# RG-LRU gates in rows of their own, the attention's mixed rows in its idle buffers, the residual rows loaded one projection sooner

## The chip, the cores and the metric

The kernel runs on one core of a Trainium2 chip. The metric is the time of one execution on the device, in microseconds (us). The core's engines each run their own queue of instructions in order and meet through semaphores: PE (TensorE, the matmuls), DVE (VectorE), ACT (ScalarE), POOL (GpSimd) and SP (SyncE, which here issues nearly all DMAs).

## The reference

One inference step of a small decoder trunk: 2 layers, model width 1024, one prompt of 1024 tokens and 8 sample tokens that go on from caches. Each layer is one input projection, three mixers side by side, one output projection and a layer norm. In short:

```python
proj = x @ w_in                               # q, k, v, gates, lru, ssd inputs
q, k, v, g_att, x_lru, g_lru, z_ssd, xbc, dt = split(proj)
br_a = sliding_window_attention(q, k, v, sinks) * silu(g_att)     # 512 wide
xl   = causal_conv(x_lru)
r, ig = sigmoid(xl @ w_a + b_a), sigmoid(xl @ w_x + b_x)          # 8 blocks of 96
log_a = -8 * softplus(-lam) * r
h    = scan(exp(log_a), sqrt(1 - exp(2 * log_a)) * ig * xl)       # RG-LRU
br_b = h * silu(g_lru)                                            # 768 wide
y    = ssd_scan(silu(causal_conv(xbc)), softplus(dt + bias)) + d * x_ssd
br_c = rms_norm(y * silu(z_ssd))                                  # 768 wide
x    = layer_norm(alpha * x + concat(br_a, br_b, br_c) @ w_out)
```

## The kernel before

All activations stand transposed: channels on the 128 partitions, tokens along the row. The work goes in four steps, layer 0 and 1 by two halves of the prompt: half 0 has 512 tokens, half 1 has 512 and the 8 samples (520, computed as two chunks of 260). Float32 products are made of three matmuls with split operands (`mac3`, L301 to L303: high by high, high by low, low by high). A weight block comes in by `W8`: a load (L250), a split on ACT (L226 in half 0, L253 in half 1) and a low part on POOL (L227), or, in half 1, a load of the low part kept from half 0 (L252).

A step projects, block by block of 128 channels (`project`): k and v, dt, then four times q, the attention gate and two SSD blocks, then eight SSD blocks, then the RG-LRU blocks as XL 0 to 2, GL 0 to 2, XL 3 to 5, GL 3 to 5 (`lru_project`; GL is the gate path, whose tanh is L345 and product L346 in `gate_silu`). Attention, SSD and RG-LRU themselves run as streams of small pieces between the projections (`spawn`, `pump`). Their results, the mixed rows, go to DRAM (`mixd`, four groups of 512 channels). `out_proj` reads them group by group in the order attention (0), SSD (3), RG-LRU (1), the rest (2): `load_mix` loads four rows of a group and splits each into a high part (L233, ACT) and a low part (L234, DVE). For each group PE makes eight out tiles, and DVE adds each to the residual rows r (L1024).

The tiles in question: a u tile is 4 rows of 520 floats on each partition (`u_tile`, pool of NU = 10), used for x, for conv results (xc, xb, zc), for gates, for mixed rows, for r and for the norm. Tiles "qa" (4 of them) hold the split queries, "sp" (4) scores and transposed probabilities; both lie idle when the attention of a step has ended. In half 1, `ssd_stream` also takes the 8 samples through the SSD one by one (`sample`): B and C of two samples come broadcast as "bb" (L685), the state as h0 (L687, 2 buffers), ACT scales (L689), POOL updates the state (L690, L691), DVE reduces it (L694). `finish` (L595, L597) makes an SSD block's gated result, `squares` (L608 on ACT, L609 on DVE) its sum of squares for the norm, which ends with a ones matmul (L731). The gate matmuls of the RG-LRU are L455, its scan L471, and its gated result L483.

The order of each engine's instructions is fixed when the kernel is built, by the scheduler of the tile framework, from the order of the code, the sizes of the pools and its own estimates of time; a tile of a pool can be written only when the last reader of the slot's former tile is done. On SP all loads and stores stand in one such order.

Of the kernel before, what the change touches and what calls it, by code (L numbers as in the profile page):

```python
# [12 lines left out]
F32R = mybir.dt.float32r  # L13
AF = mybir.ActivationFunctionType
# [3 lines left out]
P = 128  # L18
# [3 lines left out]
NS = 8  # L22
# [12 lines left out]
NH = 5  # L35
NS2 = 4
NE = 5
NU = 10
NQ = 2
ND = 4  # L40
NA = 3
# [9 lines left out]
def tile_trunk(ctx, tc, outs, x_t, cache_k, cache_v, st_lru_conv, st_ssd_conv, st_ssd_h, w_in, w_dt, w_out,  # L51
# [23 lines left out]
    def u_tile(dt=F32):  # L75
        return up.tile([P, 4, WMAX], dt, tag="u", name="u")
# [4 lines left out]
    def wtile(shape, tag, bufs=1, dt=F32):  # L81
        return wk.tile(shape, dt, tag=tag, name=tag, bufs=bufs)
# [259 lines left out]
    def gate_silu(ps, W, out):  # L342

        th = wtile([P, WMAX], "ev", NE)
        S.activation(sv(th[:, :W], W), pv(ps, W), AF.Tanh, scale=0.5)  # L345
        V.scalar_tensor_tensor(sv(out, W), sv(th[:, :W], W), 1.0, pv(ps, W), op0=ALU.add, op1=ALU.mult)  # L346
# [60 lines left out]

    def lru_project(st, l, half, x, j, what):  # L410

        W = HALF + NS * half
        if what == 0:
            xc = st["xc", j] = u_tile()
        else:
            gt = st["gt", j] = u_tile()
        for i in range(3):
            t = 3 * j + i
            if what == 0:
                ps = project(l, x, W, B_XL + t)  # L420
                conv(ps, half, W, lru_p[:, t, :], l * LS + 32, past_l[:, l, t, :], halo_l[:, t, :], xc[:, i, :W],
                     last_l[:, :, t])
                dma(xc[32 * i:32 * i + 32, 3, :W], xc[96:P, i, :W])
                if half and t == 5:
                    spawn("tail", rows_out(last_l.rearrange("p c t -> p (c t)"), 66, (
                        (0, 18, p_lru_conv[l, 0].rearrange("c (t p) -> (c t) p", p=P)),
                        (18, 66, s_lru_conv[l, :, 2, :].rearrange("b (t p) -> b t p", p=P)))), 2)
            else:
                ps = project(l, x, W, B_GL + t)
                gate_silu(ps, W, gt[:, i, :W])  # L430
            st["lru", j, what, i] = True

    def lru_stream(st, l, half, mixrows):
# [3 lines left out]
        for j in range(2):  # L437
# [5 lines left out]
            for i in range(3):  # L443
                while ("lru", j, 1, i) not in st:
                    yield 1
                t = 3 * j + i
                gate = st["gt", j][:, i, :W]
                r, ig = wtile([P, WMAX], "hb", NH), wtile([P, WMAX], "hb", NH)
                for gi, dst in ((0, r), (1, ig)):
                    for cs in chunks(W):  # L450
# [134 lines left out]
    def ssd_stream(st, l, half, mixrows):  # L585
# [81 lines left out]
        def sample(g):  # L667
# [12 lines left out]
            ysum = wtile([P, 3, NS], "ysum")  # L680
            heads = slice(6 * g, 6 * g + 6)
            for b in range(NS):
                if b % 2 == 0:
                    bb = wtile([P, 2, 2, P], "bb", 2)
                    dma(bb, bview(bcd, b * 2 * P, [[0, P], [1, 4 * P]]))  # L685
                h0, u = wtile([P, 3, P], "h0", 2), wtile([P, 3, P], "sd", ND)
                dma(h0, st_ssd_h[l, b, heads].rearrange("(t e) p n -> (e p) t n", e=2))  # L687
                for t in range(3):
                    S.activation(u[:, t, :], bb[:, b % 2, 0, :], AF.Copy, scale=dcols[:, 0, t, b:b + 1])  # L689
                G.tensor_tensor(h0, h0, dcols[:, 1, :, b:b + 1].to_broadcast([P, 3, P]), ALU.mult)  # L690
                G.tensor_tensor(h0, h0, u, ALU.add)  # L691
                dma(s_ssd_h[l, b, heads].rearrange("(t e) p n -> (e p) t n", e=2), h0)
                for t in range(3):
                    V.tensor_tensor_reduce(u[:, t, :], bb[:, b % 2, 1, :], h0[:, t, :], 1.0, 0.0,  # L694
                                           op0=ALU.mult, op1=ALU.add, accum_out=ysum[:, t, b:b + 1])
                yield 1
            finish(g, cs, NS, ysum)
# [113 lines left out]
    def attention_q(st, l, half, x, g):  # L811
        W = HALF + NS * half
        ps = project(l, x, W, B_Q + g)
        qa = st["qg", g] = [wtile([P, HALF], "qa", 2 * NQ, F32R) for _ in range(2)]

        def queries(q):

# [154 lines left out]


    def load_mix(half, mixd, g):
        W = HALF + NS * half
        mh, ml = u_tile(F32R), u_tile(F32R)
        for k in range(4):
            load_split(mh[:, k, :W], ml[:, k, :W], mixd[g][k * P:(k + 1) * P, :W])
        return mh, ml

    GROUPS = ((0, ("att",)), (3, ("ssd", "ssd_sub")), (1, ("lru",)), (2, ()))

    def out_proj(l, half, mixd, load_next, first):
        W = HALF + NS * half
        n = W // 2
        r = [u_tile() for _ in range(2)]
        for i in range(2):
            dma(r[i][:, :, :W], xd[l, half][512 * i:512 * i + 512, :W].rearrange("(k p) w -> p k w", p=P))
        cur = first
        for gi, (g, _) in enumerate(GROUPS):  # L990
            if gi == 1 and half == 0:
# [15 lines left out]
            for part in ((slice(HALF // 2, W), slice(0, HALF // 2)) if split_c else (None,)):  # L1007
                for op in range(4):
                    w = weights((l, g, op))
                    for oo in range(2):  # L1010
# [6 lines left out]
                            products = [pc(ps, W, c) for c in range(len(chunks(W)))]  # L1017
                        for out, cs in products:
                            for k in range(4):
                                mac3(out, w.part(k, slice(oo * P, oo * P + P)), mh[:, k, cs], ml[:, k, cs],  # L1020
                                     k == 0, k == 3)
                        ro, po = r[o // 4][:, o % 4, :W], pv(ps, W)
                        ro, po = (ro[:, part], products[0][0]) if part else (sv(ro, W), po)
# [89 lines left out]
    def step(l, half, x, load_next):  # L1113
# [24 lines left out]
        spawn("lru", lru_stream(st, l, half, mixrows))  # L1138
        if start:
            dma(ln_p, ln_cols)  # L1140
        for j in range(2):
            lru_project(st, l, half, x, j, 0)
            if j:
                drain("att")
                first = load_mix(half, mixd, 0)
            lru_project(st, l, half, x, j, 1)
        return out_proj(l, half, mixd, load_next, first)

    steps = [(l, half) for l in range(LAYERS) for half in range(2)]
    for l, half in steps:  # L1150
# [137 lines left out]
```

## Time and profile before

| | |
|---|---|
| time, median of 3 runs | 1694.64 us (1694.28 to 1696.47) |
| the profiled execution's own time | 1691.48 us |
| its span in the trace | 1689.7 us |
| PE busy | 1580.7 us (94%) |
| DVE, ACT, POOL busy | 63%, 57%, 34% of the span |
| mean bandwidth of the DMA queues | 200 GB/s |

The profiled execution is one run; a duration of the trace belongs to it and not to the median. The busy shares are means over four steps: what an engine is worth at one place is read from the waits there. PE's clock is granted at full or at half speed; the windows show it as a share of full speed.

### The profile page before, as it was taken

How to read it: one execution, taken by the hardware profiler on the slowest of the kernel's cores; microseconds unless marked ns; L12 is line 12 of the kernel's file. 1: busy time of each engine (PE TensorE's matmuls, PEld its weight loads, DVE VectorE, ACT ScalarE, POOL GpSimd, SP SyncE). 2: the span in 40 equal slices, each digit the busy share in tenths (PEclk: the TensorE clock that was granted, in tenths of full speed). 3: DMA queues.
4: the chain of work that ended last, by engine and by line, in shares of the span. 5: the costliest groups of instructions: out<-in, count | busy, mean ns of one | idle time of the engine just before them, and what ended most of it. 6: DMA issues, size and time to landing. Idle time of an engine off the chain costs nothing.

```text
span 1689.7 us, 30520 instructions
## 1 busy us (share of the span) xinstructions
PE 1580.7 (94%) x10696; PEld 1344.8 (80%) x10696; DVE 1071.8 (63%) x2118; ACT 964.2 (57%) x2066; POOL 578.5 (34%) x642
## 2 busy tenths in 40 slices
PE   8899998999989989989998999988999998989896
PEld 6677776688889888779976777656889997978896
DVE  5656667855944756774487565679436558577724
ACT  5655566733555746783256555667346656477724
POOL 4543665342010344300144436654412105352000
PEclk9999999999999999999999999999999999999999
DMA  8655554976564766687646555559866456565966
GB/s 274 192 169 162 152 173 156 316 244 200 146 190 150 216 188 200 194 291 251 198 129 194 163 162 152 153 183 306 251 213 197 157 175 199 179 209 183 310 200 207
DMA packets 210657, 337.40 MB, mean 200 GB/s; under 512 B 24116, under 2 KB 64000, under 8 KB 210456
## 3 DMA queue, kind: packets, MB, share of 16 engines
q1 hardware_dynamic: 208200, 331.27, 62.0%
q10 hardware_dynamic: 2304, 4.20, 0.7%
q8 instruction: 84, 1.38, 0.3%
q14 instruction: 69, 0.57, 0.1%
HBM read 242.76 MB, written 92.05 MB: 198 GB/s over the span
## 4 chain that ended last, share of the span: by engine, by line
PE 58%; DVE 15%; DMA 12%; ACT 7%; issue 4%; SPq 2%; POOL 2%; DVEq 0%; ACTq 0%; POOLq 0%
PE ip L301 16%; PE ip L303 16%; PE ip L302 16%; PE mm L879 2%; DMA wraw<-in_w_in_dram 2%; DMA wl<-low 2%; DVE u L360 2%; PE mm L655 1%; PE mm L850 1%; DMA acr<-acsd 1%; PE mm L868 1%; PE mm L455 1%; DVE hb L471 1%; DMA out_dram<-h 1%; DMA bb<-bcd 1%
## 5 line engine op out<-in xcount | busy, mean ns | idle before, releaser
L301 PE MATMUL ip<-u,wh 128*128 128x260 f32 (+3 forms) x2592 | 857.8, 331 | 53.4 <-DVE u L346 18.7
L303 PE MATMUL ip<-u,wl 128*128 128x260 f32 (+3 forms) x2592 | 844.1, 326 | 7.3 <-DMA wl<-low 7.1
L302 PE MATMUL ip<-u,wh 128*128 128x260 f32 (+3 forms) x2592 | 842.2, 325 | 0.0
L301 PEld LDWEIGHTS ip<-u,wh 128*128 128x128 f32 x2592 | 497.6, 192 | 114.8 <-DVE u L346 22.8
L303 PEld LDWEIGHTS ip<-u,wl 128*128 128x128 f32 x2592 | 496.3, 192 | 54.8 <-DMA wl<-low 9.4
L302 PEld LDWEIGHTS ip<-u,wh 128*128 128x128 f32 x2592 | 497.4, 192 | 38.4 <-issue 2.7
L227 POOL TENSOR_TENSOR wl<-wraw,wh 128x512 fp32r<-128x512 f32 x216 | 310.2, 1439 | 330.2 <-ACT wh L226 263.8
L253 ACT ACTIVATE wh<-wraw 128x512 fp32r<-128x512 f32 x224 | 138.1, 625 | 175.2 <-PE ip L302 138.7
L226 ACT ACTIVATE wh<-wraw 128x512 fp32r<-128x512 f32 x216 | 135.2, 627 | 167.7 <-PE ip L302 99.1
L1024 DVE SCALAR_TENSOR_TENSOR u<-u,ip 128x512 f32<-128x512 f32 (+3 forms) x136 | 89.2, 657 | 165.0 <-PE ip L303 164.0
L360 DVE SCALAR_TENSOR_TENSOR u<-ev,ssd_p,u 128x512 f32<-128x512 f32 x120 | 100.7, 839 | 24.6 <-ACT u L353 22.2
L638 ACT ACTIVATE cq<-acr 128x384 f32<-128x384 f32 x56 | 29.3, 523 | 107.1 <-DMA acr<-acsd 83.6
L858 ACT ACTIVATE sp<-sp,mx 128x257 f32<-128x257 f32 (+1 forms) x128 | 62.4, 490 | 37.4 <-DVE mx L854 37.3
L639 POOL TENSOR_TENSOR cq<-cq,u 128x384 f32<-128x384 f32 x56 | 61.7, 1104 | 50.6 <-ACT cq L638 39.1
L645 ACT ACTIVATE acr<-acr,acs 128x128 f32<-128x128 f32 x192 | 62.8, 392 | 25.8 <-POOL acr L642 25.2
L360 DVE SCALAR_TENSOR_TENSOR u<-ev,lru_p,u 128x512 f32<-128x512 f32 x72 | 63.0, 874 | 18.3 <-ACT u L353 18.0
L234 DVE TENSOR_TENSOR u<-u 128x512 fp32r<-128x512 f32 (+1 forms) x88 | 64.0, 754 | 16.6 <-ACT u L233 16.6
L233 ACT ACTIVATE u<-u 128x512 fp32r<-128x512 f32 (+1 forms) x88 | 51.7, 626 | 35.6 <-DVE sd L595 15.9
L647 DVE TENSOR_TENSOR acr<-acr,q 128x384 f32<-128x384 f32 x64 | 41.2, 676 | 48.4 <-ACT q L633 41.5
L455 PE MATMUL mm<-u,gw 96*32 96x260 f32 (+1 forms) x576 | 56.6, 472 | 12.0 <-ACT q L629 5.4
L854 DVE CUSTOM_DVE_ANT_0 sp<-mm,amask,sp 128x256 f32<-128x256 f32 (+1 forms) x128 | 54.5, 463 | 15.3 <-PE mm L851 13.1
L690 POOL TENSOR_TENSOR h<-h,dcols 128x384 f32<-128x384 f32 x32 | 30.6, 959 | 83.7 <-DMA h<-in_st_ssd_h_dram 43.7
(282 smaller groups left out, 2130.9 us busy)
## 6 DMA issues: line engine op xcount, KB each, us to landing
wraw<-in_w_in_dram SPq DMA_DIRECT2D x304, 256.0 KB
wl<-low SPq DMA_DIRECT2D x224, 256.0 KB
low<-wl SPq DMA_DIRECT2D x216, 256.0 KB
wraw<-in_w_out_dram SPq DMA_DIRECT2D x136, 256.0 KB
acr<-acsd SPq DMA_DIRECT2D x64, 192.0 KB
u<-mixd SPq DMA_DIRECT2D x32, 260.0 KB
u<-mixd SPq DMA_DIRECT2D x32, 256.0 KB
mixd<-u SPq DMA_DIRECT2D x24, 260.0 KB
```

The lines of the kernel that those rows point to most:

```text
L226: S.activation(dh, src, AF.Copy)
L227: G.tensor_tensor(dl, src, dh.bitcast(F32), ALU.subtract)
L234: V.tensor_tensor(dl, raw, dh.bitcast(F32), ALU.subtract)
L253: S.activation(h, raw, AF.Copy)
L301: PE.matmul(out, wh, xh, start=first, stop=False)
L302: PE.matmul(out, wh, xl, start=False, stop=False)
L303: PE.matmul(out, wl, xh, start=False, stop=last)
L360: V.scalar_tensor_tensor(out[:, :HALF], raw[:, t:t + HALF], prm[:, wo + t:wo + t + 1], out[:, :HALF], op0=ALU.mult, op1=ALU.add)
L455: PE.matmul(ps[c0:c1, :n], gw[:, gi, k, b0:b0 + c1 - c0], xc[:96, k, cs], start=True, stop=True, skip_group_check=True)
L645: S.activation(acr[i][:, e, :], acr[i][:, e, :], AF.Exp, scale=-1.0, bias=nacs[:, eb + 3 * i + e:eb + 3 * i + e + 1])
L858: S.activation(s[:, kv, :nk + 1], s[:, kv, :nk + 1], AF.Exp, scale=-1.0, bias=mx[:, kv:kv + 1], accum_out=den[:, kv:kv + 1])
L1024: V.scalar_tensor_tensor(ro, ro, ALPHA if gi == 0 else 1.0, po, op0=ALU.mult, op1=ALU.add)
```

## The change

- The gates of the RG-LRU no longer lie three to a u tile. Each is a row tile of its own, "gt", with 5 buffers (`NG`).
- The pool of u tiles has 9 slots instead of 10.
- `load_mix` of group 0 (the attention's mixed rows) takes its high parts from the four "qa" tiles and its low parts, into which it loads, from the four "sp" tiles. The other groups keep two u tiles.
- The two loads of the residual rows r move out of `out_proj` into `load_rows`, which is called before the last GL projection.
- In `sample`, bb holds one sample instead of two, with two buffers as before, so that a load is half the size and there are twice as many.

```diff
-NU = 10
+NU = 9
+NG = 5
...
-    def lru_project(st, l, half, x, j, what):
+    def lru_project(st, l, half, x, j, what, before_last=None):
...
-            gt = st["gt", j] = u_tile()
+            gt = st["gt", j] = []
         for i in range(3):
             t = 3 * j + i
+            if i == 2 and before_last:
+                before_last()
...
                 ps = project(l, x, W, B_GL + t)
-                gate_silu(ps, W, gt[:, i, :W])
+                gt.append(wtile([P, WMAX], "gt", NG))
+                gate_silu(ps, W, gt[i][:, :W])
...
-                gate = st["gt", j][:, i, :W]
+                gate = st["gt", j][i][:, :W]
...
-                if b % 2 == 0:
-                    bb = wtile([P, 2, 2, P], "bb", 2)
-                    dma(bb, bview(bcd, b * 2 * P, [[0, P], [1, 4 * P]]))
+                bb = wtile([P, 2, P], "bb", 2)
+                dma(bb, bview(bcd, b * 2 * P, [[0, P], [1, 2 * P]]))
...
-        qa = st["qg", g] = [wtile([P, HALF], "qa", 2 * NQ, F32R) for _ in range(2)]
+        qa = st["qg", g] = [wtile([P, WMAX], "qa", 2 * NQ, F32R)[:, :HALF] for _ in range(2)]
...
-        mh, ml = u_tile(F32R), u_tile(F32R)
+        if g == 0:
+            mh = [wtile([P, WMAX], "qa", 2 * NQ, F32R) for _ in range(4)]
+            ml = [wtile([P, WMAX], "sp", NS2, F32R) for _ in range(4)]
+        else:
+            mh, ml = ([u[:, k, :] for k in range(4)] for u in (u_tile(F32R), u_tile(F32R)))
         for k in range(4):
-            load_split(mh[:, k, :W], ml[:, k, :W], mixd[g][k * P:(k + 1) * P, :W])
+            load_split(mh[k][:, :W], ml[k][:, :W], mixd[g][k * P:(k + 1) * P, :W])
...
-    def out_proj(l, half, mixd, load_next, first):
+    def load_rows(l, half):
+
         W = HALF + NS * half
-        n = W // 2
         r = [u_tile() for _ in range(2)]
         for i in range(2):
             dma(r[i][:, :, :W], xd[l, half][512 * i:512 * i + 512, :W].rearrange("(k p) w -> p k w", p=P))
+        return r
...
+    def out_proj(l, half, mixd, load_next, first, r):
...
-            lru_project(st, l, half, x, j, 1)
-        return out_proj(l, half, mixd, load_next, first)
+            lru_project(st, l, half, x, j, 1, (lambda: rows.extend(load_rows(l, half))) if j else None)
+        return out_proj(l, half, mixd, load_next, first, rows)
```

Lines of the changed kernel have other numbers: most are 1 to 4 higher around the RG-LRU and SSD (L233 becomes L234, L345 L346, L455 L459, L608 L612, L685 L688), and L1024 becomes L1036.

The scheduler's order changes with it. On ACT, where the last GL projection of the first step begins, there stood, from the conv's output of the last XL block to the gate's tanh:

```order
L353 ACTIVATE u<-ip,lru_p 128x512
L233 ACTIVATE u<-u 128x512 x4
L226 ACTIVATE wh<-wraw 128x512
L608 ACTIVATE ev<-u 128x512 x3
L226 ACTIVATE wh<-wraw 128x512
L345 ACT_TABLE_LOAD
L345 ACTIVATE ev<-ip 128x512
```

And at the same place of the changed kernel:

```order
L354 ACTIVATE u<-ip,lru_p 128x512
L227 ACTIVATE wh<-wraw 128x512
L612 ACTIVATE ev<-u 128x512 x3
L227 ACTIVATE wh<-wraw 128x512
L346 ACT_TABLE_LOAD
L346 ACTIVATE ev<-ip 128x512
```

The four splits of the mixed rows are gone from here; they stand among the last SSD projections now (`qa<-sp`). On PE, inside the last GL projection of the first step, the ones matmul of the norm (L731) and a batch of gate matmuls (L455) stood between its matmuls:

```order
L301 MATMUL ip<-u,wh 128x512
L302 MATMUL ip<-u,wh 128x512
L731 MATMUL mm<-ssq,ones 128x512
L455 MATMUL mm<-u,gw 32x512 x8
L303 MATMUL ip<-u,wl 128x512
L301 MATMUL ip<-u,wh 128x512
```

In the changed kernel they stand ahead of that projection's first matmul (here behind the end of the one before it):

```order
L303 MATMUL ip<-u,wh 128x512
L304 MATMUL ip<-u,wl 128x512
L734 MATMUL mm<-ssq,ones 128x512
L459 MATMUL mm<-u,gw 32x512 x8
L302 MATMUL ip<-u,wh 128x512
L303 MATMUL ip<-u,wh 128x512
```

On PE in the second step (half 1), where out_proj begins, two batches of gate matmuls stood ahead of the second and of the third out tile (24 matmuls each):

```order
L303 MATMUL ip<-u,wl 128x260
L455 MATMUL mm<-u,gw 32x260 x16
L301 MATMUL ip<-u,wh 128x260
...
L303 MATMUL ip<-u,wl 128x260
L455 MATMUL mm<-u,gw 32x260 x16
L301 MATMUL ip<-u,wh 128x260
```

In the changed kernel the first batch is divided over these two places, and the second comes in three pieces behind the fourth, fifth and sixth tile:

```order
L304 MATMUL ip<-qa,wl 128x260
L459 MATMUL mm<-u,gw 32x260 x11
L302 MATMUL ip<-qa,wh 128x260
...
L304 MATMUL ip<-qa,wl 128x260
L459 MATMUL mm<-u,gw 32x260 x5
L302 MATMUL ip<-qa,wh 128x260
```

## Rows read from the trace of the kernel before

T1 to T4 are the places where the last GL projection of a step meets `out_proj`, in the first to the fourth step.

**Rows 1.** The page, its first part: busy us (share of the span) xinstructions by engine.

```profile
PE 1580.7 (94%) x10696; PEld 1344.8 (80%) x10696; DVE 1071.8 (63%) x2118; ACT 964.2 (57%) x2066; POOL 578.5 (34%) x642
```

**Rows 2.** The waits of PE: who waited for whom, us in total, times, longest.

```profile
PE ip L301 <- DVE u L346: 18.7, 8, 6.3
...
PE ip L301 <- DVE u L1024: 10.4, 9, 3.6
```

**Rows 3.** ACT in order of time, T1: start, us, instruction, [idle before <-releaser].

```profile
285.17 2.19 ACT L233 ACTIVATE u<-u 128x512 fp32r<-128x512 f32 x4 [4.65 <-DVE sd L595]
...
287.79 1.65 ACT L608 ACTIVATE ev<-u 128x512 f32<-128x512 f32 x3
...
289.98 1.28 ACT L345 ACT_TABLE_LOAD   x1
291.28 0.60 ACT L345 ACTIVATE ev<-ip 128x512 f32<-128x512 f32 x1
```

**Rows 4.** DVE in order of time, T1.

```profile
283.02 0.68 DVE L483 SCALAR_TENSOR_TENSOR u<-hb,u 128x512 f32<-128x512 f32 x1
...
284.28 0.86 DVE L595 SCALAR_TENSOR_TENSOR sd<-u,dcol,mm 128x128 f32<-128x128 f32 x3
...
286.18 0.55 DVE L597 TENSOR_TENSOR u<-sd,u 128x384 f32<-128x384 f32 x1
...
287.92 1.89 DVE L234 TENSOR_TENSOR u<-u 128x512 fp32r<-128x512 f32 x3
289.72 2.35 DVE L609 TENSOR_TENSOR ssq<-ssq,ev 128x512 f32<-128x512 f32 x2
292.00 0.68 DVE L346 SCALAR_TENSOR_TENSOR u<-ev,ip 128x512 f32<-128x512 f32 x1
```

**Rows 5.** PE in order of time, T1.

```profile
292.73 0.79 PE L301 MATMUL ip<-u,wh 128*128 128x512 f32 x1 [6.34 <-DVE u L346]
...
298.87 1.05 PE L731 MATMUL mm<-ssq,ones 128*128 128x512 f32 x2
...
301.70 0.50 PE L303 MATMUL ip<-u,wl 128*128 128x512 f32 x1
```

**Rows 6.** Waits for a slot, and the lines L233 and L988.

```profile
ACT u L233 <- DVE sd L595: 15.9, 4, 4.7
...
L233 ACT ACTIVATE u<-hb x8: 623/626/629, 341.9 to 361.2; 128x520 fp32r<-128x520 f32 x8
...
  DVE u L1024: 0.9, 1
```

**Rows 7.** Windows: us, busy by engine (instructions), granted clock, DMA share, GB/s.

```profile
292.73:299.10 6.37, 6.37 (x15) 5.00 (x16) 1.72 (x2) 2.32 (x4) 3.97 (x4) 0.52 0.90 278
340.00:400.00 60.00, 59.92 (x258) 47.95 (x257) 27.90 (x35) 19.22 (x32) 26.43 (x21) 1.00 0.74 239
745.03:749.50 4.47, 4.47 (x24) 4.47 (x25) 3.81 (x7) 4.01 (x9) 0.54 (x1) 0.62 1.04 382
```

**Rows 8.** PE in order of time, T2.

```profile
740.43 1.96 PE L455 MATMUL mm<-u,gw 96*32 96x260 f32 x32
745.03 0.40 PE L301 MATMUL ip<-u,wh 128*128 128x260 f32 x1 [2.64 <-DVE u L1024]
```

**Rows 9.** PE in order of time, at T3 and T4.

```profile
1132.19 0.79 PE L301 MATMUL ip<-u,wh 128*128 128x512 f32 x1 [6.34 <-DVE u L346]
...
1579.62 0.58 PE L301 MATMUL ip<-u,wh 128*128 128x260 f32 x1 [3.61 <-DVE u L1024]
```

**Rows 10.** A weight load on SP's queue at T1, and who waited for L685.

```profile
291.56 0.34 SPq L250 DMA_DIRECT2D wraw<-in_w_out_dram  x1
...
  ACT sd L689: 16.2, 6
```

**Rows 11.** DVE and PE in order of time, sample stage of the second step.

```profile
596.79 0.90 DVE L694 CUSTOM_DVE_ANT_0 sd<-bb,h 128x128 f32<-128x128 f32 x1 [1.94 <-POOL h L691]
...
601.50 0.91 PE L879 MATMUL mm<-sp,vtok 128*64 128x128 f32 x6 [4.88 <-DVE sd L595]
```

More of the change, by code (lines that the diff above doesn't have):

```diff
@@ L688, in sample @@
                 for t in range(3):
-                    S.activation(u[:, t, :], bb[:, b % 2, 0, :], AF.Copy, scale=dcols[:, 0, t, b:b + 1])
+                    S.activation(u[:, t, :], bb[:, 0, :], AF.Copy, scale=dcols[:, 0, t, b:b + 1])
                 G.tensor_tensor(h0, h0, dcols[:, 1, :, b:b + 1].to_broadcast([P, 3, P]), ALU.mult)
@@ L693, in sample @@
                 for t in range(3):
-                    V.tensor_tensor_reduce(u[:, t, :], bb[:, b % 2, 1, :], h0[:, t, :], 1.0, 0.0,
+                    V.tensor_tensor_reduce(u[:, t, :], bb[:, 1, :], h0[:, t, :], 1.0, 0.0,
                                            op0=ALU.mult, op1=ALU.add, accum_out=ysum[:, t, b:b + 1])
@@ L975, in load_mix @@
         W = HALF + NS * half
-        mh, ml = u_tile(F32R), u_tile(F32R)
+        if g == 0:
[3 more added lines that the diff above has]
+            mh, ml = ([u[:, k, :] for k in range(4)] for u in (u_tile(F32R), u_tile(F32R)))
         for k in range(4):
-            load_split(mh[:, k, :W], ml[:, k, :W], mixd[g][k * P:(k + 1) * P, :W])
+            load_split(mh[k][:, :W], ml[k][:, :W], mixd[g][k * P:(k + 1) * P, :W])
         return mh, ml
-    GROUPS = ((0, ("att",)), (3, ("ssd", "ssd_sub")), (1, ("lru",)), (2, ()))
-    def out_proj(l, half, mixd, load_next, first):
+    def load_rows(l, half):
         W = HALF + NS * half
-        n = W // 2
         r = [u_tile() for _ in range(2)]
@@ L988, in out_proj @@
             dma(r[i][:, :, :W], xd[l, half][512 * i:512 * i + 512, :W].rearrange("(k p) w -> p k w", p=P))
+        return r
+    GROUPS = ((0, ("att",)), (3, ("ssd", "ssd_sub")), (1, ("lru",)), (2, ()))
+    def out_proj(l, half, mixd, load_next, first, r):
+        W = HALF + NS * half
         cur = first
@@ L1019, in out_proj @@
                             for k in range(4):
-                                mac3(out, w.part(k, slice(oo * P, oo * P + P)), mh[:, k, cs], ml[:, k, cs],
+                                mac3(out, w.part(k, slice(oo * P, oo * P + P)), mh[k][:, cs], ml[k][:, cs],
                                      k == 0, k == 3)
@@ L1140, in step @@
             dma(ln_p, ln_cols)
+        rows = []
         for j in range(2):
```

## The prediction

> **What bounds the kernel now.** The page comes first. TensorE is busy 1580.7 us, 94% of the span [rows 1]. The change leaves PE's work as it is, so a gain can only come out of PE's idle time, or out of stretches at the lower clock. The profiled execution took 1691.48 us against a median of 1694.64 us; the sum is made against 1691.48, and the 3.2 us are added at the end.
>
> The waits of PE come next [rows 2]. Among the largest totals stand the gate's product L346 (18.7 us in 8 waits) and the residual sum L1024 (10.4 us in 9). Both belong to the place where the last GL projection of a step meets out_proj; I call these places T1 to T4, one for each step.
>
> T1 shows the mechanism. ACT works in order. From 280.52 us on (285.17 - 4.65) it stands at the split L233 of the attention's mixed rows, whose tile is an old u slot, until DVE's L595 has read that slot for the last time at 285.14 (284.28 + 0.86) [rows 3, 4]. Behind the four L233 stand the squares L608, a table load and the tanh L345, which ends at 291.88; DVE's L346 ends at 292.68, and PE, idle for 6.34 us, restarts at 292.73 [rows 3 to 5]. ACT spent 15.9 us in four such waits, one in each step [rows 6]. DVE was not idle meanwhile: its scan chain ended at 283.70 with L483, and four lows L234 (the last three 1.89 us) and two sums of squares L609 (2.35 us) stood ahead of L346 [rows 4]. Then PE runs at about half clock: 6.37 us at a granted 0.52 [rows 7].
>
> In the wide half (T2) the long wait comes later: PE is in out_proj already, runs a batch of gate matmuls of 1.96 us, and then waits 2.64 us for L1024 [rows 8].
>
> **The change, part by part.**
>
> *The split out of the way (T1, T3).* In the new order the split (now L234) and DVE's lows are gone from this place. What is late next: the squares need DVE's last product of the SSD, L597, which ended at 286.73 (286.18 + 0.55) [rows 4] and stays where it was. From there three squares (1.65), a weight split (0.60, taken as long as the tanh), the table load (1.28) and the tanh (0.60) [rows 3] end at 290.86, and the product behind it (0.68 [rows 4]) at 291.54. So only 1.1 of the 6.34 us come back by this way. But the ones matmul and a batch of gate matmuls, which cut the last GL projection in two from 298.87 to 301.70, 2.8 us [rows 5], now stand ahead of it. They need the last sum of squares. In the new order one conv product (0.68) and three sums follow the SSD's product; from 287.4 on, at 0.63 us each (a third of the three L234) to 1.17 (half of the two L609) [rows 4], they end between 289.3 and 290.9. Add 2.8, and the projection starts between 292.1 and 293.7, and has no cut. Before, it started at 292.73 and lost 2.83 in the cut, as if it had started at 295.56. The gain is 1.8 to 3.4 us; I take 2.5 at T1 and 2.5 at T3, which has the same 6.34 us [rows 9]. Lower end: 1.1, if the small matmuls only change places. Upper end: the whole 6.3, if the squares don't bind, and the half-clock loss (0.48 of 6.37 us, 3.1) with it: 9.4.
>
> *Gate matmuls spread (T2, T4).* Of the two batches ahead of the third out tile one now goes in pieces between later tiles. The tile comes 1.96 us sooner by the batch, and by up to 2.64 by the wait, which was for DVE, whose queue loses four lows a little ahead. That is 4.6 us at this tile [rows 8]. The pieces come back behind it, where PE's later waits for DVE can take them in; I take 4.0, so that a third of the batch stays on the path. Ends: 0, if the wait only comes back behind the pieces; and 4.6 with the 1.7 us of the clock (0.38 of the 4.47 us at 0.62 [rows 7]), 6.3. At T4 the wait is 3.61 us [rows 9]; I take 4.0 too, ends 0 and 7.3 (one more by the longer wait).
>
> *Residual rows sooner.* DVE waited for them 0.9 us, once in all [rows 6]; between 0 and 0.9, I take 0. The cost is on SP. In the new order the second load of them stands ahead of the out weights and waits for the slot that L597 frees at 286.73. Before, the next out weight was issued at 291.56 [rows 10], which leaves 4.8 us of cover; without it, those weights come later by what the load is late.
>
> *Attention's mixed rows.* Four loads, four ACT splits (2.19 us) and four lows (0.63 each) [rows 3, 4] run far sooner, among the last SSD projections, which hide them. On a chain there they would cost 2.2 + 2.5 = 4.7 us per step; I take 0.
>
> *Gates in rows of their own, nine u slots.* The same instructions, other tiles. With a slot fewer the next step's x waits for one: its splits out of hb ended at 361.2 us in the first step at the latest [rows 6]. PE is in out_proj without a wait until 400 at least [rows 7], so 38 us cover a delay. I take 0, and a loss only beyond that cover.
>
> *Sample rows of B and C.* 16 loads of 256 KB become 32 of 128 KB, with two samples held instead of four. A load's issue takes SP 0.34 us [rows 10]: 5.4 us in all, off the path unless SP is late. ACT waited for these loads 16.2 us in 6 places, 2.7 each [rows 10]. But in the stretch that PE ends up waiting for, DVE's reduce waited for POOL's L691, not for bb, and PE waited 4.88 us behind it [rows 11]; the state h0 had only two buffers already, so samples two apart were tied to each other before. From a loss of 21.6 us per layer (8 samples by 2.7) to a gain of 4.9; I take 0, because the row nearest to PE's wait names POOL.
>
> Against this part stands a rule of the Trainium skill, page "DMA: Bandwidth & Descriptors", section "Anatomy of one DMA": a DMA costs about 2.0 us fixed, and its bytes at 436 GB/s, so that by an estimate two of 128 KB need 4.6 us where one of 256 KB needs 2.6. Its figure was measured for DMAs issued by GpSimd; the 2.7 us of the row agree with its 2.6. By that rule, with each of 16 added fixed costs on the path, the change would cost 32 us, and the sum would come to 1714 us.
>
> **Sum.** 2.5 + 4.0 + 2.5 + 4.0 = 13.0 us; 1691.5 - 13.0 = 1678.5, and with the 3.2 us to the median about 1681.5 us, 0.8% less. A measurement of this kernel can tell about 0.2%, 3.4 us, from no change.
>
> **The rivals.**
>
> *The waits only move (0 to 8 us gained).* For it: the squares still hold ACT at T1, which leaves 5.2 of 6.3 us, and DVE works through nearly all of that wait [rows 4], so that what leaves one queue is soon behind another. Against it: the small matmuls go into the hole, whatever holds PE there. Twice 1.1 and 1 from the wide steps together: 3 us, 1691 us.
>
> *More than the waits (20 to 30 us).* T1 to T4 come near their upper ends, 6 us each, and the sample stage gives 2 per layer: 28 us, 1667 us. For it: 3.1 and 1.7 us of clock loss hang on these waits [rows 7]. Against it: the clock fell to 0.62 behind a wait of only 2.64 us [rows 7, 8], and by my sum T1 still has some 3 us or more in one piece.
>
> *Slower.* The loads of the sample rows stand in SP's queue behind the reduces of two samples before, and the weights stand behind them. A new wait costs 2.7 us, as the old ones did. Five of eight samples in each layer: 10 x 2.7 = 27 us against the 13.0, 1681.5 + 27 = 1708 us. It decides from five new waits in both layers together (13.0 / 2.7). For it: SP is the one queue for nearly all loads, and bb was awaited before. Against it: the reload of h0 already paces the samples. The rule of the Trainium skill above is this rival with each added load on the path.
>
> **Numbers.** Forecast (8 to 20 us gained) 0.50; waits only move 0.20, half of it within 0.2%; more 0.15; slower 0.15, of which 0.04 ends within 0.2%. So faster 0.75, same 0.14, slower 0.11. The range of 1667 to 1694 us leaves out most of the slower rival and the far end of "more", some 0.18 together, and holds the T1 to T4 terms from one end to nearly the other; the likeliest case alone has 1674 to 1687.
>
> **What would show it.** Right: no wait of ACT for L595 ahead of a split at the four places; at T1 PE restarts with the ones and gate matmuls, and the last GL projection ends 2 to 3 us sooner; the third out tile of T2 starts near 741 instead of 745 us; no wait for the residual rows. Wrong: SP standing at the sample rows while PE waits for weights; a wait of PE behind the samples longer than 4.88 us; ACT waiting for x at the start of a step.

## The result, and the profile after

The changed kernel takes 1712.23 us (median of 4 runs, 1707.08 to 1714.33), the kernel before, run beside it, 1695.56 us. The ratio is 1.0091, with a 95% interval of 1.0070 to 1.0111: 0.9% slower, where I had forecast 0.8% faster. (Ratios and intervals here come from the single runs, so they differ a little from the quotient of two medians, which is 1.0098.) The profiled execution has a span of 1712.4 us, 22.7 us above the one before. That one, at 1691.48 us, was 4 us under the median of its kernel, so differences of two traces come out some microseconds larger than the ratios say.

The page's first part of the changed kernel answers to [rows 1]:

```profile
PE 1588.0 (93%) x10696; PEld 1343.5 (78%) x10696; DVE 1073.5 (63%) x2118; ACT 965.7 (56%) x2068; POOL 573.1 (33%) x642
```

PE is busy 7 us longer for the same number of matmuls, so some 15 of the 22.7 us are idle time. Its waits answer to [rows 2] (us in total, times, longest):

```profile
PE ip L302 <- DVE u L1036: 19.9, 14, 3.2
PE ip L304 <- DMA wl<-low: 19.1, 4, 12.0
PE mm L459 <- ACT q L633: 9.5, 4, 4.1
PE mm L734 <- DVE ssq L613: 9.0, 3, 4.2
...
PE mm L459 <- ACT q L707: 5.7, 3, 3.8
```

The gate's product, which had 18.7 us as L346, is gone from the largest waits, as forecast. In its place stand the residual sum (19.9 against 10.4), the low part of a weight block (12.0 us in one piece; a "low weight" below), and ACT's copies and the sums of squares.

To see where the time goes, the k-th projection matmul of one trace is set against the k-th of another (each has 7776, in the same order), and the gain or loss is summed over stages. This table is worked out from the traces, in us against the profiled execution of before, plus for a loss; e1 to e15 are the experiments below. One run each: a us or two may be chance.

```
stage                      after    e1     e3     e7    e14    e15
step 1, LRU to GL 4         +5.6   +6.5   +0.6   +5.2   +0.5  +15.5
step 1, GL 5, att. group    -3.1   -1.9   -0.0   -1.5   -0.8   -5.4
step 1, rest of out_proj    +3.9   +1.9   +0.6   +1.4   +5.6   +5.7
step 2, LRU to GL 4         +6.8   +5.5   +4.3   +2.1   +2.3  +20.3
step 2, GL 5, att. group    -4.7   -4.8   +0.2   -4.8   -0.0  -10.6
step 3, LRU to GL 4         +4.6   +6.6   +1.4   +4.4   +1.6  +16.1
step 3, GL 5, att. group    -1.7   -3.0   +0.4   -2.1   +0.4   -5.0
step 4, first 18 blocks    +15.0   +3.0   +0.8   +1.4  +16.3  +16.1
step 4, LRU to GL 4         -0.4   +2.1   +2.8   -0.1   +0.0  +17.9
step 4, GL 5, att. group    -4.1   -1.6   -0.8   -4.3   -1.0   -9.9
```

(GL 0 to GL 5 count the GL blocks of a step; "att. group" is the first group of out_proj, eight out tiles. The first 18 blocks are k, v and the four rounds of q, attention gate and two SSD blocks. No stage left out moves by more than 3.5 us.) Three places lose: the LRU stages, the rest of out_proj in step 1, and the start of step 4, where 15 us go at once.

The LRU rows of steps 1 and 3 need care. They end where GL 5 starts, and the ones and gate matmuls, which stood inside GL 5, now stand ahead of it. GL 4 and GL 5 together take 3.3 us less than before in step 1 and 1.9 us less in step 3; the GL 5 rows of steps 2 and 4 show 4.7 and 4.1 us less. That is 14.0 us at the four places, where the prediction had 13.0. The change gained what it was to gain, and lost some 37 us of the trace's span elsewhere.

At T1, PE in order of time, against [rows 5]:

```profile
294.43 1.96 PE L734 MATMUL mm<-ssq,ones 128*128 128x512 f32 x2 [4.23 <-DVE ssq L613]
...
319.90 0.50 PE L302 MATMUL ip<-qa,wh 128*128 128x512 f32 x1 [2.90 <-DVE u L1036]
...
325.83 0.77 PE L302 MATMUL ip<-qa,wh 128*128 128x512 f32 x1 [2.90 <-DVE u L1036]
```

PE waits for the sums of squares now, and L346's wait is gone; but two waits for L1036 of 2.90 us each have come up behind. The windows of the small matmuls and of GL 5 in the changed kernel (columns as in [rows 7]):

```profile
294.43:298.98 4.55, 4.55 (x18) 0.91 (x18) 1.37 (x2) 4.40 (x7) 3.57 (x3) 0.62 0.84 259
298.98:304.64 5.66, 5.66 (x28) 4.62 (x25) 5.33 (x5) 5.59 (x7) 0.00 (x0) 1.00 0.55 170
```

The lower clock behind PE's wait now falls on the small matmuls, which take 4.55 us at a granted 0.62 instead of 2.83 us at 0.99. GL 5 runs whole at 1.00 in 5.66 us; before, it took 8.55 us without the cut, most of it at the 0.52 of [rows 7].

DVE in the same stretch, against [rows 4]:

```profile
292.09 2.28 DVE L613 TENSOR_TENSOR ssq<-ssq,ev 128x512 f32<-128x512 f32 x3
...
317.35 0.69 DVE L470 SCALAR_TENSOR_TENSOR hb<-hb 128x512 f32<-128x512 f32 x1 [2.48 <-ACT hb L468]
317.96 0.68 DVE L473 SCALAR_TENSOR_TENSOR hb<-hb 128x512 f32<-128x512 f32 x1
318.56 0.68 DVE L235 TENSOR_TENSOR u<-u 128x512 fp32r<-128x512 f32 x1
319.16 0.68 DVE L1036 SCALAR_TENSOR_TENSOR u<-u,ip 128x512 f32<-128x512 f32 x1
...
323.40 1.68 DVE L235 TENSOR_TENSOR u<-u 128x512 fp32r<-128x512 f32 x1
325.01 0.67 DVE L1036 SCALAR_TENSOR_TENSOR u<-u,ip 128x512 f32<-128x512 f32 x1
```

The three sums took 0.76 us each, near the short end of my bounds. Then, before the L1036 that PE needs, DVE's order has an LRU product, which waits 2.48 us for ACT's square root (L468), and the low part (L235) of a mixed row of the next group, and before the second one a scan and two lows. The split gone from ahead of the tanh has been followed by others ahead of the residual sums. On ACT the waits moved as well: the 15.9 us for L595 [rows 6] are gone, and ACT now stands 27.1 us in 9 places for loads of the later groups' mixed rows, against 3.7 us in 5 before.

### The profile page after: what moved, and what is told of

Same layout as the page of the kernel before. It is cut to its first block, busy times and chain, and to the rows that moved or that the text cites. A ratio compares the mean times of both kernels' runs of the same rounds, so it can differ in the third digit from the quotient of the medians.

```text
span 1712.4 us, 30539 instructions
## 1 busy us (share of the span) xinstructions
PE 1588.0 (93%) x10696; PEld 1343.5 (78%) x10696; DVE 1073.5 (63%) x2118; ACT 965.7 (56%) x2068; POOL 573.1 (33%) x642
## 5 line engine op out<-in xcount | busy, mean ns | idle before, releaser
L302 PE MATMUL ip<-u,wh 128*128 128x260 f32 (+3 forms) x2400 | 792.6, 330 | 23.9 <-ACT wh L227 6.6
L304 PE MATMUL ip<-u,wl 128*128 128x260 f32 (+3 forms) x2400 | 780.1, 325 | 19.5 <-DMA wl<-low 19.1
L303 PE MATMUL ip<-u,wh 128*128 128x260 f32 (+3 forms) x2400 | 778.3, 324 | 0.0
L302 PEld LDWEIGHTS ip<-u,wh 128*128 128x128 f32 x2400 | 460.7, 192 | 79.1 <-issue 12.6
L304 PEld LDWEIGHTS ip<-u,wl 128*128 128x128 f32 x2400 | 460.0, 192 | 59.4 <-DMA wl<-low 20.5
L303 PEld LDWEIGHTS ip<-u,wh 128*128 128x128 f32 x2400 | 460.0, 192 | 34.3 <-issue 2.0
L228 POOL TENSOR_TENSOR wl<-wraw,wh 128x512 fp32r<-128x512 f32 x216 | 305.3, 1417 | 340.7 <-ACT wh L227 268.6
L1036 DVE SCALAR_TENSOR_TENSOR u<-u,ip 128x512 f32<-128x512 f32 (+3 forms) x136 | 88.9, 656 | 156.4 <-PE ip L304 156.2
L459 PE MATMUL mm<-u,gw 96*32 96x260 f32 (+1 forms) x576 | 63.5, 485 | 20.8 <-ACT q L633 9.5
L302 PE MATMUL ip<-qa,wh 128*128 128x260 f32 (+1 forms) x192 | 65.2, 339 | 15.5 <-DVE u L1036 15.2
L235 DVE TENSOR_TENSOR u<-u 128x512 fp32r<-128x512 f32 (+1 forms) x72 | 53.3, 770 | 20.9 <-ACT u L234 20.8
L697 DVE CUSTOM_DVE_ANT_0 sd<-bb,h 128x128 f32<-128x128 f32 x96 | 39.3, 456 | 40.1 <-POOL h L694 40.0
```

Source lines behind the costliest of these rows:

```text
L228: G.tensor_tensor(dl, src, dh.bitcast(F32), ALU.subtract)
L235: V.tensor_tensor(dl, raw, dh.bitcast(F32), ALU.subtract)
L302: PE.matmul(out, wh, xh, start=first, stop=False)
L303: PE.matmul(out, wh, xl, start=False, stop=False)
L304: PE.matmul(out, wl, xh, start=False, stop=last)
L459: PE.matmul(ps[c0:c1, :n], gw[:, gi, k, b0:b0 + c1 - c0], xc[:96, k, cs], start=True, stop=True, skip_group_check=True)
```

## The experiments

All times are medians of 4 to 12 runs; the ratio is against runs of before beside them, whose median moved between 1698 and 1699 us in these hours. Any edit makes the scheduler draw up a new order for every engine. Two edits that were to be neutral, e5 and e17, gave 1.0006 and 1.0016, so a difference of that size says little.

The theories in the expectations: A is the missing u slot, B the one-sample loads, C the moved mixed and residual rows. From e5 on, D (depth: how many samples are held) and F (number of loads) divide B, and G, from e16 on, is A at the last norm.

**e1: gates back in u tiles, ten slots; the rest of the change stays.**

```diff
-NU = 9
+NU = 10
...
-            gt = st["gt", j] = []
+            gt = st["gt", j] = u_tile()
...
```

> The changed kernel with the gates back in u tiles and the tenth u slot back; mixed rows in idle buffers, early residual rows and one-sample loads of B and C stay. Theory A (the missing u slot costs the time, by ACT waiting for a slot of the last norm at the start of the fourth step and by x splits that come four at a time): the 12 us wait of PE for a low weight near 1302 us goes, the two 1.8 us waits near 365 and 390 us go, and the time is 1692 to 1699 us. Theory B (one-sample loads of B and C cost it): 1708 us or more. Theory C (the moved mixed rows and residual rows cost it, by DVE's order in out_proj): 1705 us or more, with PE's two waits of 2.9 us near 317 and 323 us still there.

Measured 1710.89 us, 1.0077 [1.0057, 1.0097]. Of the waits that theory A names most went (the low weight's is 3.42 us instead of 12.01, and of the two of 1.8 us one is left, 1.86 us at 353 us), but the time stayed. Theory A alone falls.

**e2: as e1, with two-sample loads again** (what is left: mixed rows, residual rows).

> As the kernel with gates in u tiles and ten slots, and the loads of B and C for two samples again; what is left of the change is the mixed rows in idle buffers and the early residual rows. Theory A: within 3 us of the one with one-sample loads. Theory B: faster than that one by 8 us or more, near 1695 us. Theory C: within 3 us of it and slower than before by 10 us or more.

1698.84 us, 1.0011 [0.9994, 1.0028]. Theory B: 12 us of e1 are the one-sample loads. ACT's waits for bb are 14.0 us in 5 places, much as before. Theory C falls, as e2 is not slower than before by 10 us.

**e3: before, with one-sample loads and nothing else.**

```diff
-                if b % 2 == 0:
-                    bb = wtile([P, 2, 2, P], "bb", 2)
-                    dma(bb, bview(bcd, b * 2 * P, [[0, P], [1, 4 * P]]))
+                bb = wtile([P, 2, P], "bb", 2)
+                dma(bb, bview(bcd, b * 2 * P, [[0, P], [1, 2 * P]]))
```

> The kernel before with one change, loads of B and C for one sample. Theory A: within 4 us of before, 1692 to 1699 us. Theory B: slower by 10 us or more (each added load awaited costs 2 to 2.7 us, 16 of them 32 to 43 us at the most). Theory C: as theory A.

1708.28 us, 1.0062 [1.0038, 1.0086], some 10 us over before. Theory B again. Who waited for bb, in e3 and then in the changed kernel, against 16.2 us in 6 places [rows 10]:

```profile
  ACT sd L688: 49.3, 24
```

```profile
  ACT sd L692: 45.4, 21
```

In e3, step 2's second group of samples, ACT in order of time, then SP's loads of bb, then PE:

```profile
646.21 0.99 ACT L688 ACTIVATE sd<-bb,dcols 128x128 f32<-128x128 f32 x3 [5.45 <-DMA bb<-bcd]
...
658.07 0.98 ACT L688 ACTIVATE sd<-bb,dcols 128x128 f32<-128x128 f32 x3 [6.40 <-DMA bb<-bcd]
659.69 0.98 ACT L688 ACTIVATE sd<-bb,dcols 128x128 f32<-128x128 f32 x3 [0.64 <-DMA bb<-bcd]
660.59 0.97 ACT L645 ACTIVATE acr<-acr,acs 128x128 f32<-128x128 f32 x3
661.46 0.25 ACT L703 ACTIVATE q<-mm 128x128 f32<-128x128 f32 x1
```

```profile
651.82 0.48 SPq L684 DMA_DIRECT2D bb<-bcd  x1
...
653.47 0.38 SPq L684 DMA_DIRECT2D bb<-bcd  x1
```

```profile
661.77 4.22 PE L455 MATMUL mm<-u,gw 96*32 96x260 f32 x26 [4.06 <-ACT q L703]
```

ACT stands 6.40 us at L688 for the load that was issued at 651.82, and 0.64 us more for the one issued at 653.47; behind them come the decay factors L645 and the copy of the state L703, and PE's gate matmuls, which need what that copy frees, start 4.06 us late. PE's waits for this copy come to 7.9 us in e3, 8.5 in e1 and 5.7 in the changed kernel; before, in e2 and in e5 there is none above 0.5 us in all. SP stands too, but far less: its waits to issue bb until a reduce is done grew from 1.7 us in 4 places to 6.3 in 5.

**e5: before, one-sample loads in four buffers** (`wtile([P, 2, P], "bb", 4)`): 32 loads, and four samples held as before.

> The kernel before with one-sample loads of B and C, but four buffers, so that four samples are held as before (32 loads of 128 KB, the same memory). Theory D (depth: a load can only be issued when the reduce two samples back is done, so that ACT stands for each of them): ACT's waits for bb go from 49 us in 24 places back to some 10 to 20 us, and the time to within 4 us of before. Theory F (the fixed cost of each of the 16 added loads): ACT's waits stay above 35 us and the time stays 7 us or more above before.

1699.57 us, 1.0006 [0.9990, 1.0022], and ACT's waits:

```profile
  ACT sd L688: 12.8, 4
```

So it is the depth and not the count: 32 loads of half the size cost nothing that can be measured when four samples are held. Theory F falls. With it falls the estimate from the Trainium skill, page "DMA: Bandwidth & Descriptors", section "Anatomy of one DMA", in which the fixed cost of every added DMA was on the path.

**e6: before, B and C of all eight samples in one u tile**, four loads at once.

> The kernel before with B and C of all eight samples of a group in one u tile, loaded by four loads of two samples each at once. Theory D: ACT's waits for bb fall under 8 us (16.2 before), and the time by up to 5 us under before, if a u slot is free there in time. Rival: the u slot it takes delays other users of the pool (x, r, mixed rows), and the time is the same or up to 10 us longer. Theory F: within 3 us of before, as the count of loads is the same.

1692.09 us, 0.9959 [0.9941, 0.9977]: with e11, which contains it, the only version faster than both kernels. ACT's wait for these loads is only a little smaller than before, not under 8 us as I had expected, so the size of the gain is not explained by it:

```profile
ACT sd L691 <- DMA u<-bcd: 12.9, 4, 5.1
```

In the table's way of counting it gains in the stages with the samples of the first group, -5.0 us in step 2 and -6.0 in step 4. PE's wait of [rows 11] had been there, 8.9 us in these two steps together, and in e6 it is gone.

**e7: before, with the mixed rows of the attention in idle buffers and nothing else.**

> The kernel before with one change, the attention's mixed rows in the attention's buffers and so their split far sooner (residual rows at the old place, gates in u tiles, two-sample loads, ten u slots). If the mixed rows by themselves give the gain forecast at T1 to T4 and lose it in out_proj by DVE's order: PE's waits of 6.3 us at T1 and T3 fall to some 4 us, new waits for L1036's like appear behind, and the time is within 4 us of before. If the early residual rows are what loses it: 1683 to 1690 us against before near 1696.

1697.33 us, 0.9994 [0.9979, 1.0008]. The first reading holds. DVE's rows ahead of a wait of PE of 4.05 us at T1, and that wait:

```profile
315.76 0.69 DVE L469 SCALAR_TENSOR_TENSOR hb<-hb 128x512 f32<-128x512 f32 x1 [2.48 <-ACT hb L467]
...
318.37 0.69 DVE L235 TENSOR_TENSOR u<-u 128x512 fp32r<-128x512 f32 x1 [1.31 <-ACT u L234]
318.97 0.68 DVE L1036 SCALAR_TENSOR_TENSOR u<-u,ip 128x512 f32<-128x512 f32 x1
```

```profile
319.71 0.79 PE L302 MATMUL ip<-qa,wh 128*128 128x512 f32 x1 [4.05 <-DVE u L1036]
```

ACT's waits for loads of the later groups' mixed rows are here already, 12.4 us in 11 places.

**e8: before, with only the residual rows sooner.**

> The kernel before with one change, the residual rows loaded ahead of the last GL projection. DVE waited only 0.9 us for them before, so no gain: within 3 us of before. If their slot on SP's queue costs (the second load waits for a u slot with the out weights behind it): 4 to 10 us slower, with PE waiting for weights (wh or wl) near 310 us.

1701.95 us, 1.0021 [1.0005, 1.0037]: nothing gained, perhaps some 3 us lost. No trace shows where.

**e4: the changed kernel, decay load one yield later** (a yield ends a piece of its stream).

```diff
+            yield 7
+            if half:
                 for e in range(2):
                     dma(dcols[64 * e:64 * e + 64].rearrange("p a b c -> p (a b c)"),
                         bview(sdd, e * 96, [[0, 64], [1, 96]]))
-            yield 7
```

> The changed kernel with the load of the sample decays (dcols) written one yield later, so that in the fourth step two low weights and two raw weights are issued on SP ahead of it. Theory A in its form for the fourth step (SP stands at that load while the weights behind it are awaited): the 12 us wait of PE near 1302 us falls to 5 us or less and the half clock behind it shortens, 1697 to 1705 us. If the wait has another cause (ACT late with the weight splits, the loads themselves slow), it stays above 9 us and the time within 4 us of the changed kernel's.

1710.97 us, 1.0084 [1.0066, 1.0103]; PE's wait is 8.31 us, between the two readings. The order of SP there makes up a part of the wait, and the time is not changed by more than chance: the start of step 4 still loses 14.8 us.

**e9: the changed kernel, whole, with e6's edit; e10: that, with the residual rows at their old place; e11: e7 and e6 together.**

> The changed kernel, whole, but with B and C of all eight samples in one u tile (nine slots stay), loaded by four loads of two samples. Theory D (only the depth of the sample loads made the change slow): 1690 to 1699 us, 12 us or more under the changed kernel, ACT's waits for these loads under 20 us. If the gate rows and the ninth slot cost as well, hidden in the first runs behind the sample loads: 1702 us or more, with PE's wait of some 8 to 12 us for a low weight near 1300 us still there.

> As the kernel before it in this list, with the residual rows loaded at the start of out_proj again. If the early rows cost some 3 us, as the run with them alone suggests (1.0021 of before): 2 to 5 us faster than with them. If that was chance: within 2 us.

> The kernel before with the attention's mixed rows in idle buffers and the sample rows in one u tile of ten. The sample rows alone gave 0.9959 of before. If the mixed rows' gain at T1 to T4 is only given back by DVE's order in out_proj, the time is that of the sample rows alone, 1688 to 1695 us; if they add to it: under 1687 us.

e9 1716.19 us, 1.0110 [1.0082, 1.0138]; e10 1719.00 us, 1.0130 [1.0104, 1.0156]; e11 1694.88 us, 0.9971 [0.9951, 0.9990]. With nine slots the tile for the samples seems to take one that the sample's attention needs for its cache. PE's waits in e9 fit that (the wait for the cache is there in e9 and e10, and not with the ten slots of e6 and e11), and show a low weight's wait of 12.6 us:

```profile
PE mm L936 <- DMA u<-in_cache_k_dram: 17.4, 2, 8.8
PE ip L304 <- DMA wl<-low: 16.9, 4, 12.6
```

So e9 mixes two things and settles neither; early rows were no loss in this company (e10, not faster without them). In e11 the mixed rows add nothing to e6.

**e12 to e15: gate rows and nine slots taken apart.** e12 is the changed kernel with two-sample loads and, for room, four gate rows (`NG = 4`); e13 has the four rows alone; e14 is before with four gate rows and nine slots only; e15 is before with `NU = 9` only.

> The changed kernel with two-sample loads of B and C (four samples held) and, to make room, four gate rows instead of five; nine u slots. If the depth of the sample loads alone makes the change slow: 1694 to 1702 us. If gate rows and nine slots cost too, by PE's wait for a low weight at the start of the fourth step: that wait is 8 to 13 us, and the time 1704 us or more.

> Control of the one before: the changed kernel with four gate rows, and the one-sample loads kept. If the fifth row matters little: within 4 us of the changed kernel, 1708 to 1716 us. The difference to the one before is then the price of the one-sample loads among gate rows and nine slots, 8 to 14 us by the depth theory.

> The kernel before with gate rows (four) and nine u slots only. If these two cancel: within 4 us of before. If they cost by the start of the fourth step: 5 to 12 us slower with a wait for a low weight of 8 us or more near 1300 us. If they gain and only lose in company: faster by 3 us or more.

> The kernel before with nine u slots and nothing else, the gates still in u tiles. The slots are then short by one for the same users: slower than before by 8 us or more, with ACT or DVE waiting for slots in out_proj or at the start of the fourth step. If within 3 us of before, the tenth slot was spare.

| | two-sample loads | one-sample loads |
|---|---|---|
| mixed and residual rows moved, gates in u tiles, ten slots | e2 1.0011 [0.9994, 1.0028] | e1 1.0077 [1.0057, 1.0097] |
| the same, four gate rows, nine slots | e12 1.0078 [1.0058, 1.0099] | e13 1.0106 [1.0085, 1.0127] |

e14 has 1.0095 [1.0073, 1.0117], 17 us over before, where the most I had expected was 12; e15 has 1.0293 [1.0269, 1.0317]. Gate rows with nine slots cost about as much as the one-sample loads, and the two together less than the sum: e13 is only 4 us slower than e12, where I had expected 8 to 14. The tenth slot was not spare: without it, and with the gates still in u tiles, the kernel loses 50 us; the gate rows give back about two thirds of that. The table shows which: in e15 each step loses 15 to 20 us in its LRU stage and wins 5 to 11 back in the next, in e14 it loses at most 2.3 there, but the 16 us at the start of step 4 stay.

That place tells nine slots from ten in every trace that has the last norm as it was. With nine slots (the changed kernel, e4, e9, e10, e12 to e15) step 4 loses 14.5 to 16.3 us over its first 18 blocks; with ten (e1 to e3, e5 to e7, e11, e17) it loses 0.2 to 3.4. No run has gate rows with ten slots, but e15, with nine slots and no gate rows, loses as much there as e14.

In e14 PE's wait at the start of step 4 is there too, as it is in e12 (10.12 us):

```profile
1314.09 0.58 PE L304 MATMUL ip<-u,wl 128*128 128x260 f32 x1 [9.94 <-DMA wl<-low]
```

In the changed kernel that place reads, ACT, then SP, then PE:

```profile
1285.87 0.60 ACT L1108 ACTIVATE u<-mm 128x512 f32<-128x512 f32 x1 [3.09 <-DMA out_dram<-u]
...
1296.36 1.28 ACT L1111 ACT_TABLE_LOAD   x1
...
1297.96 1.28 ACT L532 ACT_TABLE_LOAD   x1
1299.26 0.21 ACT L532 ACTIVATE eda<-da 8x12 f32<-8x12 f32 x1
```

```profile
1299.49 0.65 SPq L535 DMA_DIRECT2D sdd<-eda  x2
...
1307.86 2.48 SPq L538 DMA_DIRECT2D dcols<-sdd  x2
1310.43 0.54 SPq L253 DMA_DIRECT2D wl<-low  x1
```

```profile
1314.24 0.58 PE L304 MATMUL ip<-u,wl 128*128 128x260 f32 x1 [12.01 <-DMA wl<-low]
```

ACT waits 3.09 us for a store of the last norm (its slot), then has more of that norm and a table load ahead of the sample's decay L532. The decays go out at 1299.49, and the loads that read them back (L538) stand on SP until 1307.86, with the low weight behind them at 1310.43; PE waits 12.01 us. SP's own waits, over the two steps with samples, name both parts:

```profile
SPq L538 <- DMA sdd<-eda: 14.3, 2, 7.2
SPq L535 <- ACT eda L532: 6.0, 2, 5.3
```

Before, the wait for the scatter was as long (7.2 us), but SP stood only 0.7 us for ACT's decays. They went out at 1283 us, 39.6 us behind the start of the step instead of 43.8, and PE waited under a us.

The other place is the x of the next step, in step 1: four lows (L235) come at once, as soon as PE has done with a tile, ahead of L1036 on DVE, and PE waits twice. DVE and PE of the changed kernel:

```profile
361.98 4.15 DVE L235 TENSOR_TENSOR u<-hb,u 128x520 fp32r<-128x520 f32 x4 [1.85 <-PE ip L303]
366.05 1.27 DVE L1036 SCALAR_TENSOR_TENSOR u<-u,ip 128x512 f32<-128x512 f32 x2
```

```profile
366.78 0.51 PE L302 MATMUL ip<-u,wh 128*128 128x512 f32 x1 [1.82 <-DVE u L1036]
...
391.18 0.50 PE L302 MATMUL ip<-u,wh 128*128 128x512 f32 x1 [1.82 <-DVE u L1036]
```

The table's runs with nine slots (after, e14, e15) lose 3.9 to 5.7 us in its third row, those with ten slots 0.6 to 1.9; but e2 and e11, with ten, lose 3.7 and 4.1 there too, so the slot is not the only thing that brings such a wait.

**e16: e14 with the last norm's rows of two blocks in one u tile; e17: before with this edit; e18: the changed kernel with it.**

```diff
-            yz = u_tile().rearrange("p a b -> p (a b)")
-            y, z = yz[:m, 0:DM], yz[:m, DM:2 * DM]
+            if b % 2 == 0:
+                yy = u_tile().rearrange("p a b -> p (a b)")
+            y = yy[:m, b % 2 * DM:b % 2 * DM + DM]
+            z = wtile([P, WMAX], "hb", NH).bitcast(mybir.dt.bfloat16)[:m, 0:DM]
```

> The kernel before with four gate rows and nine u slots, and the last norm's rows of two blocks in one u tile (the output of its square, which nobody reads, goes to an idle row tile in bfloat16), so that this norm needs half the slots. Theory G (nine slots cost by the last norm's wait for a slot at the start of the fourth step): PE's wait for a low weight there falls from 7 to 13 us to under 5, and the time from 1.0095 of before to 1.000 to 1.004. If the slots cost elsewhere, or the start of the fourth step is late for another reason: 1.006 or more.

> Control of the one before: the kernel before with the same change of the last norm, gates in u tiles and ten slots. The tenth slot was enough there, so within 3 us of before; if it is faster by more, the norm's slots cost time in the kernel before as well.

> The changed kernel, whole, with the same change of the last norm. By theory G: 1700 to 1706 us, what is left being the one-sample loads (7 to 10 us over before), and no wait above 5 us near 1300 us. If it stays at 1709 us or more, the slots are not what makes the changed kernel slow beside its sample loads.

e16 1708.64 us, 1.0063 [1.0040, 1.0085]; e17 1.0016 [1.0001, 1.0031]; e18 1711.76 us, 1.0081 [1.0059, 1.0103]. PE's wait halves in e16, but ACT still waits for a store of that norm, a tile of two blocks being free only behind both stores:

```profile
1318.92 0.58 PE L304 MATMUL ip<-u,wl 128*128 128x260 f32 x1 [5.53 <-DMA wl<-low]
```

```profile
1284.14 0.60 ACT L1100 ACTIVATE u<-mm 128x512 f32<-128x512 f32 x1 [5.31 <-DMA out_dram<-u]
```

The edit did not take the wait for a slot away as I had meant, and both times lie where I had put the case against theory G (1.006 or more for e16, 1709 us or more for e18). In e18 PE's low-weight wait fell to 4.39 us, and the loss at the start of step 4 is 11.1 us in e16 and 7.1 in e18, against 16.3 and 15.0 without the edit; but the ratios moved by 0.3 and 0.1%, and the intervals overlap. That nine slots lose 15 us of a trace at the start of step 4 is shown. That it is by the last norm's slots is argued from the rows, and how much of the time depends on it stays open.

## Why the prediction was wrong

- *Sample rows of B and C, taken as 0.* This step failed first. I read the one row nearest to PE's wait, where POOL was late, and set aside that ACT waited 2.7 us in 6 places already. Alone it costs 0.62% (e3), some 10 us. My slower rival named the right kind of wait, for a load held back by a reduce, but put it on SP's queue with the weights behind it. It is mostly ACT's queue that stands, 49 us in 24 places, with a copy behind it for which PE waits. By the rule of the Trainium skill, page "DMA: Bandwidth & Descriptors", section "Anatomy of one DMA", my estimate was 1714 us, near the measured time. That is luck: e5 excludes its reason, as with the depth kept 16 added loads cost nothing. The 2.7 us of [rows 10] did not bear the rule out either; they are a mean of waits and not the time of a load, and the 128 KB load issued at 651.82 in e3 reached ACT only at 658.07, 6.25 us later.
- *Gates in rows, nine slots, taken as 0.* This failed as well. I asked whether x would be late for PE, and had 38 us of cover; x was not late. What came late was DVE, with four lows in one piece ahead of L1036, and ACT at the start of step 4, behind the norm's tiles. The norm is among the users of u tiles that the section on the kernel before lists; the term asked about x alone. Alone 0.95% (e14, with four rows).
- *The split out of the way, 2.5 us each at T1 and T3.* The wait of 6.34 us went to 4.2 us and the small matmuls went into the hole, as worked out. The gain from GL 4 to GL 5 was 3.3 and 1.9 us, near the forecast, but in part by luck: GL 5 started 14.6 us behind GL 4 at T1, where I had 11.5 to 13.2, and made up for it by running at the full clock (1.00), 2.9 us that the term had only in its upper end. My upper bound for the sums was also a misreading: 1.17 us was the mean of one of 0.69 and one of 1.56. In e2 the same place gains 0.3 us at T1 and loses 1.0 at T3. Nor did the gain stay: e7, with this part alone, gains 3.3 and 1.9 us there and still loses 5.1 and 2.9 us over the three stages of steps 1 and 3. It loses 4.2 and 2.2 us in the out tiles of the first group, where PE waits for L1036, and 2.8 and 2.1 in the LRU projections ahead of GL 4. These follow the SSD projections to which the split moved, a part that I had put at 0; that the split is what costs there is not shown. That was the rival in which the waits only move.
- *Gate matmuls spread, 4.0 us each at T2 and T4.* Right in mechanism, and near in size: in e7 the three stages of step 2 give 3.0 us, those of step 4 6.2 us; the third out tile does not wait any more. In the changed kernel it starts 5.8 us sooner behind the start of GL 5 at T2, and 6.3 us at T4.
- *Residual rows, taken as 0.* Alone 1.0021: no gain, as said, and at most a small loss.
- *The sum.* The parts that gain and lose around T1 to T4 cancel (e2, e7). What is left are two costs that I had put at nothing with cover named; each gives 0.6 to 0.95% alone, and together with the rest 0.91%. The signs that I had named for being right came true, counted from the start of GL 4 or GL 5, and the kernel was slower all the same: they looked only at the parts that were to gain.

## What to carry to other kernels

A tile pool made smaller, or a load made to hold less, changes how far every engine that works in order can run ahead: list all users of the slot, and for each ask which queue stands while it waits and what is behind it there. A wait removed from the head of one queue is worth only what the next row in the same queue, and the queues it feeds, let through; read a few rows further before counting it. Count depth (how much work is held) apart from the number of transfers: here the depth cost 10 us, and the number nothing.

## What was not expected of the hardware

A scatter of the sample decays, two DMAs of 8 x 12 single floats, took from 1299.49 us at its issue until SP could issue the load that reads it back at 1307.86: 8.4 us for 768 bytes, and 8.0 us in the profiled run of before (1283.09 to 1291.06). Of the two sums of squares on DVE in [rows 4] one took 0.69 us and the other 1.56, with the same shape. Of the 20 in the kernel before, four took 1.2 to 1.6 us and the others 0.7; in the changed kernel all 20 took 0.68 to 0.70. No run here shows why.
